# A PEER layer in fp32 on one core: 320 instead of 352 tokens computed densely, 192 gathered, and the gathers begun beside the gate matrices

## Chip, cores and metric

The kernel runs on one core of a Trainium2 chip. The metric is the device time of one execution in microseconds. Three runs of the kernel before took 3478.0, 3478.22 and 3481.24 us; the median is 3478.22 us.

## What is computed

One decoder layer over 512 tokens of 2048 features, all in float32: two groups of attention heads, an output projection with residual, then a PEER block and a final RMSNorm. The change concerns the PEER block alone:

```python
q = (xt @ w_query).reshape(T, PEER_HEADS, 2, PEER_HALF)          # 512 tokens, 8 heads, 2 x 128
scores = jnp.einsum('thpc,hpnc->thpn', q, sub_keys)              # 128 keys per half
vals, idx = lax.top_k(scores, 16)
cand = vals[..., 0, :, None] + vals[..., 1, None, :]             # 16 x 16 sums
top_vals, top_c = lax.top_k(cand, 16)                            # 16 experts per head
experts = i1 * 128 + i2                                          # of 16384 experts
gates = softmax(top_vals)
hdn  = gelu(einsum('ted,td->te', expert_down[experts], x))       # 128 experts per token
y    = einsum('te,ted->td', gates * hdn, expert_up[experts])
```

An expert is one row of 2048 numbers in `expert_down` and one in `expert_up`; each table has 16384 rows (134 MB).

## The kernel before, in words

**Two ways through the experts.** For the first `ND` = 352 tokens the kernel computes all 16384 experts densely, as 128 tiles of 128 experts, and multiplies the hidden values by a gate matrix that is zero where a token did not choose the expert. For the last 160 tokens it gathers the chosen rows: 128 tokens as part "g", one row per partition and step (128 steps in `down`, 128 in `up`), and `NE` = 32 tokens as part "e", four experts at a time on 4 x 32 partitions (32 steps in each table). That makes 320 gather steps of 128 rows of 8 KB, 1 MB each. Every matmul that is not a transpose, a gate matrix or a score runs as three passes over fp32 values split into a high and a low half (`mm3`, lines 96 to 98); ScalarE makes the high half (line 90), VectorE or GpSimd the low one (line 91, argument `lo_on`).

**The stages**, in the order of the program:

1. Attention and output projection, up to about 950 us. Not touched.
2. Routing (lines 494 to 549): per head two query projections `pq` of 48 matmuls, scores `sc`, then on VectorE top-16 of the scores, candidate sums, top-16 of those, and a one-hot product `oh` that turns positions into expert numbers, for all four blocks of 128 tokens; GpSimd takes every second `oh` product (line 537).
3. Gate matrices (lines 570 to 615): the tokens are handled in `NGC` = 11 chunks of 32. Per group of 8 tokens VectorE writes two comparisons `o2` and `o1` (lines 602, 603), GpSimd (two groups in three) or ScalarE multiplies `o1` by the gates, TensorE makes the matrices `gm` (line 612), ScalarE copies them to a staging tile, and a chunk of 2 MB is written to HBM (`g_d`).
4. Early `down` tiles (lines 738 to 742): 18 tiles (`SPILL`), whose hidden values go to HBM and are needed last, and 10 (`HOLD`) that stay in SBUF, both with the low halves on GpSimd. A scheduler moves part of their matmuls forward into stages 2 and 3.
5. The main loop (lines 745 to 786): 32 groups of 4 tiles. Per group the gate columns `gt` are loaded, the hidden values multiplied and split, and for each of 16 output chunks of 128 features 12 matmuls `up` are summed in PSUM and added to `yacc` by VectorE (line 773). After every fourth chunk's worth of work one later `down` tile is computed, with one low half on VectorE and one on GpSimd. `gather_step` (line 641 on) is called up to 12 times per group: GpSimd issues the indirect DMA into one of three buffers `rows` (line 650), held back until a named matmul has run, and VectorE multiplies what arrived (line 654 for `down`, 662 for `up`).
6. The end: residual, RMSNorm and output in the last group.

Each engine works through its own queue in order, and the order is fixed when the program is built. So where a gather's product stands in VectorE's queue, all that stands behind it waits for that gather's landing.

## Time and profile before

| | us |
|---|---|
| median of three runs | 3478.22 |
| profiled execution, its own time | 3480.87 |
| its span, first to last instruction | 3479.1 |
| TensorE matmuls busy | 3282.0 (94%) |
| VectorE busy | 2545.0 (73%) |
| GpSimd busy | 1183.5 (34%) |
| ScalarE busy | 1180.3 (34%) |

The profiled execution is 1.8 us longer than its span, and 2.65 us longer than the median. All stretches below are in microseconds from the start of the span. In the rows PE is TensorE's matmuls, PEld its weight loads, DVE VectorE, ACT ScalarE, POOL GpSimd and SP the queue that issues plain DMAs; L91 is line 91 of the kernel. PEclk is the granted clock of TensorE, 1.00 being 2.4 GHz.

### The profile page before, as it was taken

What the parts mean: (1) busy time and instruction counts of PE and PEld (TensorE: products, weight loads), DVE (VectorE), ACT (ScalarE), POOL (GpSimd) and SP (SyncE); (2) the same over time, 40 slices, a digit from 0 to 9 for tenths busy, and PEclk for the clock granted to TensorE, in tenths of its full rate; (3) what the DMA queues carried; (4) which work ended last, traced back from release to release, by engine and by line L of the source; (5) the groups of instructions that cost most, each with busy time, mean ns of one, the idle gap of its engine ahead of it and who ended that gap; (6) DMA issues with size and microseconds to landing.
All of it is one profiled execution on the core that took longest, in us unless ns stands there. A gap on an engine that the chain in (4) does not pass through costs nothing.

```text
span 3479.1 us, 47060 instructions
## 1 busy us (share of the span) xinstructions
PE 3282.0 (94%) x18329; PEld 3015.0 (87%) x18329; DVE 2545.0 (73%) x3652; ACT 1180.3 (34%) x1651; POOL 1183.5 (34%) x584
## 2 busy tenths in 40 slices
PE   6999999999998977899999999999999999998787
PEld 4887778878877766899999899999999999998787
DVE  5236664453469999127988889999999998998775
ACT  3224443342321267333333333333333333332133
POOL 2000000000054356454544445554554555552200
PEclk9999999999999999999999999999999999999899
DMA  4222222224332134547888889899898999988763
GB/s 179 93 93 68 70 76 68 69 89 138 123 137 75 46 130 162 196 151 299 339 329 342 308 339 352 344 344 353 330 358 335 346 345 348 346 344 318 283 199 108
DMA packets 207902, 780.35 MB, mean 224 GB/s; under 512 B 19648, under 2 KB 69696, under 8 KB 163456
## 3 DMA queue, kind: packets, MB, share of 16 engines
q1 hardware_dynamic: 160752, 440.35, 36.3%
q0 software_dynamic: 46080, 335.56, 24.4%
q8 instruction: 143, 2.34, 0.3%
q10 hardware_dynamic: 848, 1.44, 0.1%
q14 instruction: 79, 0.65, 0.1%
HBM read 739.70 MB, written 36.41 MB: 223 GB/s over the span
## 4 chain that ended last, share of the span: by engine, by line
PE 22%; DMA 18%; DVE 10%; issue 8%; POOL 1%; ACT 0%; DVEq 0%; POOLq 0%; ACTq 0%; SPq 0%
DMA rows<-in_up,gidx 12%; DMA rows<-in_down,gidx 5%; PE dn L96 4%; PE dn L98 4%; PE dn L97 4%; PE up L96 3%; PE up L97 3%; PE up L98 3%; DVE rows L654 3%; DVE yg_g L662 2%; DVE ulo L763 1%; DVE lo L91 1%; DVE yacc L773 1%; POOL rows L650 1%; DVE hn L755 1%
## 5 line engine op out<-in xcount | busy, mean ns | idle before, releaser
L91 POOL TENSOR_TENSOR lo<-raw,hi 128x1024 fp32r<-128x1024 f32 x186 | 483.0, 2599 | 762.1 <-ACT hi L90 744.1
L96 PE MATMUL up<-hn,ulo 128*128 128x352 f32 x2048 | 673.3, 329 | 55.5 <-DVE ulo L763 55.3
L90 ACT ACTIVATE hi<-raw 128x1024 fp32r<-128x1024 f32 x416 | 439.3, 1057 | 771.6 <-PE dn L98 279.5
L96 PE MATMUL dn<-hn,lo 128*128 128x352 f32 x2048 | 678.1, 331 | 22.3 <-POOL lo L91 11.1
L98 PE MATMUL dn<-hn,hi 128*128 128x352 f32 x2048 | 674.8, 329 | 0.0
L97 PE MATMUL dn<-hn,hi 128*128 128x352 f32 x2048 | 674.5, 329 | 0.0
L98 PE MATMUL up<-hn,uhi 128*128 128x352 f32 x2048 | 668.8, 327 | 0.0
L97 PE MATMUL up<-hn,uhi 128*128 128x352 f32 x2048 | 666.3, 325 | 0.0
L91 DVE TENSOR_TENSOR lo<-raw,hi 128x1024 fp32r<-128x1024 f32 x230 | 316.4, 1376 | 284.7 <-ACT hi L90 284.4
L762 ACT ACTIVATE uhi<-uraw 128x1024 fp32r<-128x1024 f32 x256 | 271.4, 1061 | 640.8 <-PE up L98 597.0
L96 PEld LDWEIGHTS up<-hn,ulo 128*128 128x128 f32 x2048 | 390.2, 191 | 62.8 <-DVE ulo L763 57.8
L96 PEld LDWEIGHTS dn<-hn,lo 128*128 128x128 f32 x2048 | 387.3, 189 | 36.0 <-POOL lo L91 17.6
L662 DVE SCALAR_TENSOR_TENSOR yg_g<-rows,coef_g,yg_g 128x2048 f32<-128x2048 f32 x127 | 348.7, 2745 | 66.3 <-DMA rows<-in_up,gidx 66.2
L97 PEld LDWEIGHTS up<-hn,uhi 128*128 128x128 f32 x2048 | 389.4, 190 | 0.0
L98 PEld LDWEIGHTS up<-hn,uhi 128*128 128x128 f32 x2048 | 388.1, 190 | 0.0
L98 PEld LDWEIGHTS dn<-hn,hi 128*128 128x128 f32 x2048 | 387.6, 189 | 0.5
L97 PEld LDWEIGHTS dn<-hn,hi 128*128 128x128 f32 x2048 | 386.7, 189 | 0.6
L654 DVE SCALAR_TENSOR_TENSOR rows<-rows,hng_g 128x2048 f32<-128x2048 f32 x128 | 322.6, 2526 | 47.0 <-DMA rows<-in_down,gidx 46.9
L763 DVE TENSOR_TENSOR ulo<-uraw,uhi 128x1024 fp32r<-128x1024 f32 x256 | 315.9, 1234 | 47.8 <-ACT uhi L762 47.5
L650 POOL DMA_INDIRECT rows<-in_up,gidx x128 | 227.6, 1778 | 168.5 <-PE up L98 88.1
L773 DVE TENSOR_TENSOR yacc<-yacc,up 128x352 f32<-128x352 f32 x496 | 246.0, 509 | 38.8 <-PE up L98 38.7
L650 POOL DMA_INDIRECT rows<-in_down,gidx x128 | 229.5, 1793 | 90.1 <-issue 41.3
(258 smaller groups left out, 4885.7 us busy)
## 6 DMA issues: line engine op xcount, KB each, us to landing
raw<-in_down_t SPq DMA_DIRECT2D x256, 512.0 KB
uraw<-in_up_t SPq DMA_DIRECT2D x256, 512.0 KB
raw<-in_w_qk SPq DMA_DIRECT2D x64, 512.0 KB
g_d<-stg SPq DMA_DIRECT2D x11, 2048.0 KB
gt<-g_d SPq DMA_DIRECT2D x32, 704.0 KB
raw<-in_w_v SPq DMA_DIRECT2D x32, 512.0 KB
raw<-in_w_o SPq DMA_DIRECT2D x32, 512.0 KB
raw<-in_w_pq SPq DMA_DIRECT2D x32, 512.0 KB
```

Source lines behind the costliest of these rows:

```text
L90: A.activation(hi, raw, AF.Copy)
L91: (lo_on or V).tensor_tensor(lo, raw, hi.bitcast(F32), ALU.subtract)
L96: PE.matmul(ps, a[1], b[0], start=first, stop=False)
L97: PE.matmul(ps, a[0], b[1], start=False, stop=False)
L98: return PE.matmul(ps, a[0], b[0], start=False, stop=last)
L650: ld = G.indirect_dma_start(out=rows, out_offset=None, in_=table, in_offset=bass.IndirectOffsetOnAxis(ap=ix[:, j:j + 1], axis=0))
L654: V.scalar_tensor_tensor(rows, rows, 1.0, hng[part], ALU.mult, ALU.mult, accum_out=dots[part][:, j:j + 1])
L662: V.scalar_tensor_tensor(yg[part], rows, coef[part][:, j:j + 1], yg[part], ALU.mult, ALU.add)
L755: V.tensor_tensor(pl, hold[e], ph.bitcast(F32), ALU.subtract)
L762: A.activation(uh, raw, AF.Copy)
L763: V.tensor_tensor(ul, raw, uh.bitcast(F32), ALU.subtract)
L773: V.tensor_tensor(yacc[:, c], yacc[:, c], ps[:, :ND], ALU.add)
```

## The change

Six things change together.

- `ND` goes from 352 to 320, `NE` from 32 to 64: the dense matmuls have 320 columns, there are 10 gate chunks, and part "e" has 64 steps per table, so that there are 384 gather steps.
- Routing is done in two halves of two blocks (`RB`): first blocks 2 and 3, which hold all gathered tokens, while the query projections run; the queries of blocks 0 and 1 are kept in SBUF and routed afterwards.
- The gather code moves out of the main loop's pool, and five gather steps (`PRE`) are called after each gate chunk, without a matmul to wait for.
- Early tiles: `SPILL` goes from 18 to 28, so 38 tiles are computed ahead instead of 28.
- The main loop has 16 groups of 8 tiles (`NG`): 24 matmuls per PSUM sum, half as many additions to `yacc`. The gate columns arrive in runs of 1 KB instead of 512 B, the `up` weights still in runs of 4 KB. A gather is due 1.6 times per output chunk of 24 matmuls while `down` tiles remain, and 0.85 times after that.
- In the main loop both low halves of a `down` tile are VectorE's.

```diff
-ND = 352
+ND = 320
-NE = 32
+NE = 64
+RB = 2
-SPILL = 18
+SPILL = 28
+NG = 8
+PRE = 5
...
+        def choose(hh, b0, queries):
+            bs = slice(b0, b0 + RB)
...
+        kept = rp.tile([P, 2 * PH, RB * P], F32, name="kept")
+        def queries(hp):
+            ps = aux(f"pq{hp}")
...
+            A.copy(qt, ps[:, RB * P:])
+            A.copy(kept[:, hp], ps[:, :RB * P])
+            return qt
+        for hh in range(PH):
+            choose(hh, NB - RB, queries)
...
+        for hh in range(PH):
+            choose(hh, 0, lambda hp: kept[:, hp])
...
-                o2 = gp.tile([P, QT, P], F32, name="o2", bufs=4)
-                o1 = gp.tile([P, QT, P], F32, name="o1", bufs=4)
+                o2 = gp.tile([P, QT, P], F32, name="o2", bufs=2)
+                o1 = gp.tile([P, QT, P], F32, name="o1", bufs=3)
...
             DMA.dma_start(g_d[ch], stg)
+            for _ in range(PRE):
+                gather_step(None)
...
-            for dc in range(8):
-                raw = xp.tile([P, NG, 256], F32, tag="uraw", name="uraw", bufs=3)
+            for c in range(NK):
+                raw = xp.tile([P, NG, P], F32, tag="uraw", name="uraw", bufs=3)
...
-                        down_tile(e, (V, G))
+                        down_tile(e, (V, V))
...
-                for _ in range(1 + (dc % 2 == 0) if HOLD + g * NG < NE1 - SPILL else 1):
+                due += 1.6 if e < NE1 - SPILL else 0.85
+                while due >= 1:
                     gather_step(mm)
+                    due -= 1
```

Three places in the order of the built programs show where work is moved.

The first is VectorE's queue in the middle of the gate stage. Before, only comparisons stand there (`o1` and `o2` are the tiles of lines 602 and 603):

```order
L602 TENSOR_TENSOR o2_9343<-iota_e_9034,i2t_9046 128x1024
L603 TENSOR_TENSOR o1_9344<-iota_e_9034,i1t_9045 128x1024
L602 TENSOR_TENSOR o2_9360<-iota_e_9034,i2t_9046 128x1024
L603 TENSOR_TENSOR o1_9361<-iota_e_9034,i1t_9045 128x1024
L602 TENSOR_TENSOR o2_9386<-iota_e_9034,i2t_9046 128x1024
L603 TENSOR_TENSOR o1_9387<-iota_e_9034,i1t_9045 128x1024
```

Now products of gathered rows (`rows15` is the gather of step 15) stand between them:

```order
L512 SCALAR_TENSOR_TENSOR rows15_9721,dots_e_6975<-rows15_9721,hng_e_9435 128x2048
L670 TENSOR_TENSOR o2_9696<-iota_e_9325,i2t_9328 128x1024
L512 SCALAR_TENSOR_TENSOR rows16_9724,dots_e_6975<-rows16_9724,hng_e_9435 128x2048
L512 SCALAR_TENSOR_TENSOR rows17_9727,dots_e_6975<-rows17_9727,hng_e_9435 128x2048
L512 SCALAR_TENSOR_TENSOR rows18_9730,dots_e_6975<-rows18_9730,hng_e_9435 128x2048
L670 TENSOR_TENSOR o2_9737<-iota_e_9325,i2t_9328 128x1024
L512 SCALAR_TENSOR_TENSOR rows19_9733,dots_e_6975<-rows19_9733,hng_e_9435 128x2048
L671 TENSOR_TENSOR o1_9738<-iota_e_9325,i1t_9327 128x1024
L670 TENSOR_TENSOR o2_9754<-iota_e_9325,i2t_9328 128x1024
L671 TENSOR_TENSOR o1_9755<-iota_e_9325,i1t_9327 128x1024
L671 TENSOR_TENSOR o1_9772<-iota_e_9325,i1t_9327 128x1024
L512 SCALAR_TENSOR_TENSOR rows20_9813,dots_e_6975<-rows20_9813,hng_e_9435 128x2048
```

Seven of the 50 products stand before the first comparison, four behind the last one, and 39 between the 80 comparisons.

The second is GpSimd's queue at the same place. Before, it holds the gate products and a few low halves of early tiles; now the issues of the gathers (L507) stand among them, each waiting for a free `rows` buffer, with the products (L673) and low halves (L94) queued behind:

```order
L507 DMA rows23_9822<-in_down,gidx_e_6963 128x2048
L673 TENSOR_TENSOR o1_9796<-o1_9796,gtt_9329 128x1024
L94 TENSOR_TENSOR lo_11437<-raw_11434,hi_11436 128x1024
L507 DMA rows24_9825<-in_down,gidx_e_6963 128x2048
L507 DMA rows25_9905<-in_down,gidx_e_6963 128x2048
L507 DMA rows26_9908<-in_down,gidx_e_6963 128x2048
L673 TENSOR_TENSOR o1_9830<-o1_9830,gtt_9329 128x1024
L507 DMA rows27_9911<-in_down,gidx_e_6963 128x2048
L673 TENSOR_TENSOR o1_9871<-o1_9871,gtt_9329 128x1024
L94 TENSOR_TENSOR lo_11471<-raw_11468,hi_11470 128x1024
```

From the first gate product to the last, this queue holds 26 products and 16 low halves now. Of the matmuls of the 38 early tiles (1824), 672 stand before the tables of the gate stage are transposed, 388 between them and the last `gm`, and 764 behind the last `gm`; before, 944 of 1344 stood behind it.

The third is TensorE's queue while the queries are projected. Before, five matmuls of an early tile stand between a query projection and its scores:

```order
L98 MATMUL pq2_7227<-hn0_6788,hi_7260 128x512
L96 MATMUL dn110_9965<-hn0_6788,lo_9999 128x352
L97 MATMUL dn110_9965<-hn1_6789,hi_9998 128x352
L98 MATMUL dn110_9965<-hn0_6788,hi_9998 128x352
L96 MATMUL dn110_9965<-hn0_6788,lo_9999 128x352
L97 MATMUL dn110_9965<-hn1_6789,hi_9998 128x352
L510 MATMUL sc2_7290<-sk_6974,qt_7288 128x128 x4
L96 MATMUL pq3_7323<-hn0_6788,lo_7327 128x512
```

Now the scores, for two blocks, stand right behind the projection whose result they wait for:

```order
L99 MATMUL pq2_7192<-hn0_6788,lo_7226 128x512
L100 MATMUL pq2_7192<-hn1_6789,hi_7225 128x512
L101 MATMUL pq2_7192<-hn0_6788,hi_7225 128x512
L556 MATMUL sc22_7256<-sk_6984,qt_7253 128x128 x2
L99 MATMUL pq3_7275<-hn0_6788,lo_7279 128x512
L100 MATMUL pq3_7275<-hn1_6789,hi_7278 128x512
```

## Rows read from the trace of the kernel before

**Rows 1.** Windows: busy us (instructions) of PE, PEld, DVE, ACT, POOL, PEclk, DMA share, GB/s

```profile
0.00:953.00 953.00, 917.34 (x4375) 730.71 (x4376) 455.08 (x875) 346.02 (x563) 23.17 (x28) 1.00 0.29 97
953.00:1224.00 271.00, 247.94 (x1122) 203.98 (x1121) 226.76 (x1007) 63.41 (x78) 128.57 (x55) 0.95 0.26 87
1224.00:1403.00 179.00, 133.64 (x891) 120.19 (x890) 173.57 (x107) 124.69 (x222) 103.38 (x38) 0.92 0.37 148
1403.00:1576.00 173.00, 162.36 (x949) 156.71 (x949) 27.82 (x23) 54.38 (x70) 90.83 (x38) 0.97 0.53 173
1576.00:3171.00 1595.00, 1579.66 (x9608) 1568.82 (x9607) 1451.38 (x1369) 508.58 (x610) 805.26 (x401) 1.00 0.90 340
...
3171.00:3479.00 308.00, 241.06 (x1394) 234.61 (x1392) 210.37 (x274) 83.21 (x112) 32.32 (x24) 0.90 0.61 211
```

**Rows 2.** Windows of 100 us: 352 columns in the main loop, 512 in the attention

```profile
2300.00:2400.00 100.00, 100.00 (x614) 99.72 (x613) 92.96 (x95) 31.27 (x37) 50.27 (x25) 1.00 0.88 339
100.00:200.00 100.00, 100.00 (x430) 80.47 (x429) 24.80 (x22) 21.49 (x22) 0.00 (x0) 1.00 0.30 94
```

**Rows 3.** Windows of the main loop, for the PEld and DMA columns

```profile
2200.00:2800.00 600.00, 599.60 (x3661) 597.14 (x3661) 556.41 (x541) 193.31 (x231) 311.39 (x153) 1.00 0.91 345
1680.00:1720.00 40.00, 40.00 (x245) 39.80 (x245) 38.00 (x42) 13.53 (x17) 17.54 (x11) 1.00 1.00 381
2840.00:2860.00 20.00, 20.00 (x125) 20.00 (x124) 18.92 (x17) 8.09 (x12) 9.34 (x5) 1.00 1.02 394
```

**Rows 4.** Timeline of the last projection and its scores: start us, us, instruction

```profile
1202.32 0.40 PE L98 MATMUL pq<-hn,hi 128*128 128x512 f32 x1
...
1202.81 0.59 ACT L507 COPY qt<-pq 128x512 f32<-128x512 f32 x1 [14.79 <-PE pq L98]
...
1203.45 1.16 PE L510 MATMUL sc<-sk,qt 128*128 128x128 f32 x8
```

**Rows 5.** Groups of the gate stage, 1224 to 1403 us: busy, mean ns, idle before

```profile
L603 DVE TENSOR_TENSOR o<-iota_e,i1t 128x1024 f32<-128x1024 f32 x44 | 103.1, 2344 | 0.8 <-ACT i1t L589 0.8
...
L605 POOL TENSOR_TENSOR o<-o,gtt 128x1024 f32<-128x1024 f32 x29 | 78.7, 2712 | 66.4 <-DVE o L603 35.1 <-PE gm L612 21.9 <-PE dn L98 4.7
L602 DVE TENSOR_TENSOR o<-iota_e,i2t 128x1024 f32<-128x1024 f32 x44 | 64.1, 1458 | 0.2 <-ACT i2t L589 0.2
...
L91 POOL TENSOR_TENSOR lo<-raw,hi 128x1024 fp32r<-128x1024 f32 x8 | 24.7, 3089 | 2.8 <-ACT hi L90 2.8
```

**Rows 6.** VectorE's timeline in the main loop

```profile
2302.16 1.21 DVE L763 TENSOR_TENSOR ulo<-uraw,uhi 128x1024 fp32r<-128x1024 f32 x1
2303.29 2.28 DVE L654 SCALAR_TENSOR_TENSOR rows<-rows,hng_g 128x2048 f32<-128x2048 f32 x1
...
2305.50 2.28 DVE L654 SCALAR_TENSOR_TENSOR rows<-rows,hng_g 128x2048 f32<-128x2048 f32 x1
...
2307.71 3.42 DVE L91 TENSOR_TENSOR lo<-raw,hi 128x1024 fp32r<-128x1024 f32 x1
2311.05 2.28 DVE L654 SCALAR_TENSOR_TENSOR rows<-rows,hng_g 128x2048 f32<-128x2048 f32 x1
```

**Rows 7.** GpSimd's timeline at the same time

```profile
2306.47 3.57 POOL L91 TENSOR_TENSOR lo<-raw,hi 128x1024 fp32r<-128x1024 f32 x1 [5.83 <-ACT hi L90]
```

**Rows 8.** The gathers' DMA queue over the whole run: packets, MB, share

```profile
q0 software_dynamic: 46080, 335.56, 24.4%
```

**Rows 9.** Groups of 3171 to 3310 us, where the last 20 gathers run

```profile
L96 PE MATMUL up<-hn,ulo 128*128 128x352 f32 x176 | 63.3, 360 | 38.0 <-DVE ulo L763 37.9
...
L751 DVE TENSOR_TENSOR hold<-hold,gt 128x352 f32<-128x352 f32 x3 | 1.5, 521 | 9.1 <-DMA hold<-hid_d 9.1
```

**Rows 10.** The tile `up` on TensorE: ns, first and last start

```profile
L96 PE MATMUL up<-hn,ulo x2048: 318/325/662, 1575.8 to 3461.1; 128*128 128x352 f32 x187
```

**Rows 11.** Timelines of the last gathers: an issue, and the product that waits for its landing

```profile
3212.28 0.94 POOL L650 DMA_INDIRECT rows<-in_up,gidx  x1 [1.43 <-DVE ulo L763]
...
3220.68 2.35 DVE L662 SCALAR_TENSOR_TENSOR yg_g<-rows,coef_g,yg_g 128x2048 f32<-128x2048 f32 x1 [2.01 <-DMA rows<-in_up,gidx]
```

More of the change, by code (lines that the diff above doesn't have):

```diff
@@ L470, in peer_block @@
     hold_p = ctx.enter_context(tc.tile_pool(name="hold", bufs=HOLD))
+    ga = ctx.enter_context(tc.tile_pool(name="gath", bufs=1))
+    hng = {}
+    sel = ga.tile([P, NE], F32, name="sel")
+    V.tensor_copy(sel, ident[:, 0:NE])
+    for r in range(1, ER):
+        V.tensor_tensor(sel, sel, ident[:, r * NE:(r + 1) * NE], ALU.add)
+    steps = [(w, part, j) for part, n in (("e", EH), ("g", HK)) for w in (down, up) for j in range(n)]
+    lists = {"e": (gidx_e, gate_e), "g": (gidx, top.rearrange("p b h k -> p b (h k)")[:, GB])}
@@ new lines, in peer_block, with gather_step @@
+    dots = {p: ga.tile([P, n], F32, name=f"dots_{p}") for p, n in (("e", EH), ("g", HK))}
+    coef = {p: ga.tile([P, n], F32, name=f"coef_{p}") for p, n in (("e", EH), ("g", HK))}
+    yg = {}
+    gstep = [0]
+    def gather_step(after):
+        n = gstep[0]
+        gstep[0] += 1
+        if n >= len(steps):
+            return
+        table, part, j = steps[n]
+        ix, gate = lists[part]
+        last = j == ix.shape[1] - 1
+        if n == 0:
+            hng["e"] = ga.tile([P, D], F32, tag="hy", name="hng_e")
+            for r in range(ER):
+                DMA.dma_start(hng["e"][r * NE:(r + 1) * NE], hn_d[:NE])
+        elif part == "g" and steps[n - 1][1] == "e":
+            hng["g"] = ga.tile([P, D], F32, tag="hy", name="hng_g")
+            DMA.dma_start(hng["g"], hn_d[NE:])
+        rows = ga.tile([P, D], F32, tag="rows", name=f"rows{n}", bufs=3)
+        ld = G.indirect_dma_start(out=rows, out_offset=None, in_=table,
+                             in_offset=bass.IndirectOffsetOnAxis(ap=ix[:, j:j + 1], axis=0))
+        if after is not None:
+            tc.add_manual_dep(ld.ins, after.ins.name, PACE, reason="pace")
+        if table is down:
+            V.scalar_tensor_tensor(rows, rows, 1.0, hng[part], ALU.mult, ALU.mult, accum_out=dots[part][:, j:j + 1])
+            if last:
+                A.activation(coef[part], dots[part], AF.Gelu_apprx_tanh)
+                V.tensor_tensor(coef[part], coef[part], gate, ALU.mult)
+        elif j == 0:
+            yg[part] = ga.tile([P, D], F32, tag="hy", name=f"yg_{part}")
+            V.tensor_scalar(yg[part], rows, coef[part][:, j:j + 1], None, ALU.mult)
+        else:
+            V.scalar_tensor_tensor(yg[part], rows, coef[part][:, j:j + 1], yg[part], ALU.mult, ALU.add)
+        if table is up and last:
+            fin_part(part)
@@ L683, in fin_load @@
                     fin[b, half] = t
[L684 removed]
+            fin["row"] = ga.tile([P, D], F32, tag="rows", name="frow", bufs=3)
             DMA.dma_start(fin["row"], fin_row.broadcast_to([P, D]))
@@ L774, in peer_block @@
-                if dc % 2:
-                    e = HOLD + g * NG + dc // 2
-                    if e < NE1 - SPILL:
-                        down_tile(e, (V, G))
-                    elif e < NE1:
+                ps = aux("up")
+                for j in range(NG):
+                    mm = mm3(ps[:, :ND], (uh[:, j], ul[:, j]), pp[j], j == 0, j == NG - 1)
+                if g == 0:
+                    V.tensor_copy(yacc[:, c], ps[:, :ND])
+                else:
+                    V.tensor_tensor(yacc[:, c], yacc[:, c], ps[:, :ND], ALU.add)
```

165 lines of the change are left out of this document (59 added, 106 removed).

## The prediction

> **What bounds the kernel now.** I read the windows by stage first, then the mean steps of TensorE, then what ends the waits in the stages that the change touches. The windows [rows 1] show three regimes. From 1576 to 3171 us, where two thirds of the matmuls run, TensorE is busy 1579.7 of 1595 us at full clock; VectorE (1451 us) and the DMA engines (0.90) are close behind. Between 953 and 1576 the bound changes: routing and gate matrices fill VectorE (227 of 271 us, 174 of 179), the early tiles fill TensorE while VectorE works 28 of 173 us. In the tail TensorE is busy 241 of 308 us.
>
> A matmul's price follows its columns [rows 2]: 100 us hold 614 matmuls of 352 columns, 0.163 us each, and 430 of 512 columns, 0.2326 each. That is 0.0697 us for 160 columns, so 320 columns should take 0.163 - 32 x 0.0697 / 160 = 0.149 us.
>
> **The change, part by part.** *Dense width.* 12288 matmuls (128 tiles, 48 in `down` and 48 in `up`) save 0.0139 us each: 171 us. This is all that the change can win; everything else gives back.
>
> *Front.* Nothing changes up to 953 us.
>
> *Routing in two halves.* While the queries of blocks 2 and 3 are routed, no other matmul stands between a projection and its scores, so TensorE waits for ScalarE's copy. In the timeline [rows 4] the last matmul of a projection starts at 1202.32, the scores at 1203.45: less one step of 0.23, the gap is 0.9 us with a 0.59 us copy, some 0.6 us where only half of the columns is copied first. With two scores at 0.145 (8 in 1.16) a projection takes 48 x 0.2326 + 0.6 to 0.9 + 0.3, about 12.3 us; 16 take 198: 1151. VectorE has half of its work in these 198 us and is hidden; its last piece I put at 15 us (one head of eight in 130). The second half is VectorE's alone. All four blocks took it from the first scores (953 and one projection, 965) to 1224, 259 us, so two take 130: 1296. The 672 early matmuls that stand there (100 us) are hidden in it.
>
> *Gates.* Ahead of the first comparison stand seven gathered products, 15 us, and the transposes of the tables, 5: the gates start at 1316, 92 us later than before. Their cost is VectorE's. An undisturbed comparison is one of 1024 elements, 1.13 us [rows 6] (2302.16 to 2303.29); a product is 2.21 (2303.29 to 2305.50). But the low half that ran while GpSimd worked [rows 7] (2306.47 to 2310.04) took 3.34. The gate stage shows the same [rows 5]: 88 comparisons took 103.1 + 64.1 = 167.2 us where 88 x 1.13 = 99.4 would do, 67.8 us over, 1.83 for each of the 37 GpSimd operations (29 products, 8 low halves). Now 80 comparisons (90), 39 products (86) and 42 GpSimd operations x 1.83 (77) make 253. Waits for landings come on top: an issue is followed by its product after 8.4 us [rows 11] (3212.28 to 3220.68), and with three buffers five gathers take at least 5 x (8.4 + 2.2) / 3 = 18 us of a chunk's 25, so they fit, but GpSimd's products are queued behind issues that wait for a buffer. I take 2 us per chunk, 273 in all; the bounds are none (253) and one landing of 8.4 with one GpSimd product of 2.7 [rows 5] exposed in each chunk, 36 us a chunk (360). The gates end at 1589, the last group passes TensorE at 1595, against 1403.
>
> *Early tiles.* Behind that stand 764 matmuls. Before, 944 took 173 us [rows 1] with the clock at 0.97 and 11 us idle: 764 x 0.149 / 0.97 + 11 = 128. The main loop starts at 1723 instead of 1576: **147 us of the 171 are given back here**, for ten tiles more computed ahead and 50 gathers done.
>
> *Main loop.* 90 tiles remain; I count in rounds of 8 tiles, 11.25 of them. A round holds 768 matmuls, 114.4 us. VectorE has 25.6 products x 2.2 (57), 32 halves x 1.13 (36, no GpSimd tensor operation disturbs them now) and 32 small operations at no more than the 0.52 us of such a one [rows 9] (17): 110. The DMA engines move 16.8 MB of weights, 1.3 of gate columns and 25.6 gathers of 335.56 / 320 = 1.049 MB [rows 8], 44.9 MB. That is 392 GB/s at TensorE's pace. Before, the loop needed 345 GB/s at a share of 0.91 [rows 3]; 40 us ran at 381 with the share at 1.00 and 20 us at 394 with 1.02, and TensorE lost nothing in them. So the full engines give about 381: **117.8 us per round, set by the DMA**. Bounds: 114.4 (394 held) and 130.2 (345 stays the average). I take 117.8, nearest to the longer of the full stretches. 11.25 x 117.8 = 1325, with 15 us of idle time as before: 3063.
>
> The Trainium skill ("DMA: Bandwidth & Descriptors", section "Where 436 GB/s comes from") puts the limit of transfers between HBM and SBUF at about 358 GB/s per core. By it a round would take 125.5 us and the end would come near 3527. The 381 and 394 GB/s of the rows lie above that figure, though only over 40 and 20 us.
>
> *Tail.* 76 chunks of 24 matmuls are 272 us. Before, the tail of 308 us held 1344 `up` matmuls (219 us), 18 us behind the last one [rows 10] (3461.1 to 3479.1), and 71 us lost, 38 of them behind VectorE's low halves that stand behind gathers [rows 9]. Twenty gathers ran there, now 46 do; at half of 8.4 / 3 us exposed each (1.4) they cost 64, the wait for stored hidden values (9.1 before [rows 9]) 10, the last part 15: 89. Bounds: 71 as before, and 46 x 2.8 + 25 = 154. 3063 + 361 + 18 = **3442 us** of span, 37 less than 3479.1. The profiled execution is 1.8 us longer than its span and 2.65 over the median of the runs, so the median should come to 3441.
>
> Half as many sums to `yacc` and longer runs of the gate columns I cost at nothing: VectorE and TensorE are not the bound of a round at 117.8. If they were (110 and 114.4) they would be late next.
>
> **Rivals.**
>
> *Slower: the transfers do not keep 371 GB/s.* The gain of 37 us is gone when a round takes 37 / 11.25 = 3.3 us more, 121.1 us, 371 GB/s. Place: the three `rows` buffers in the main loop. A round at 117.8 has 4.6 us per gather, 13.8 for a buffer's turn; 8.4 + 2.2 + about 1 us to the next issue leave 2.2 us. If full DMA engines make a landing later than that (over 10.9 us), VectorE stops at the product, the low halves behind it stop, and TensorE with them. For it: 345 GB/s over 600 us is the longest stretch shown, and VectorE is within 8 us of the round. Against: in the two full stretches [rows 3] TensorE was busy throughout. At 345 to 365 GB/s a round takes 130 to 123 us, the end is 3500 to 3581. A limit that shows only in long stretches, between the 345 shown over 600 us and the 381 over 40, would give the same: at 355 to 365 GB/s 123 to 126.5 us, 3500 to 3540; I give it 0.12 of this rival's 0.25, since no row shows full engines below 381.
> The figure of the skill's section above lies in that span.
>
> *All fits.* The engines hold 394 GB/s, a round is TensorE's 114.4, 38 us less; with gates at 253 the end is 3383 to 3403. For it: TensorE's idle time is 15 us in 1595 now. Against: three engines would all be over 95% busy.
>
> *The gates are longer.* 36 us per chunk instead of 27 add 87 us: 3528. For it: GpSimd's issues wait for buffers ahead of its gate products. Against: 18 us of landings fit beside 25 us of VectorE's work in a chunk. Half of this rival would end within 0.2% of before.
>
> *No price falls with the columns.* The weight loads are busy 597 of 600 us [rows 3]; if they set the pace, the matmul stays at 0.163 and 171 us are missing: 3612. Against: at 512 columns there is one load per matmul too, and they are busy only 80% of the time [rows 2]; the busy time stretches with the matmul.
> The Trainium skill ("Perfetto Trace Analysis", section "Identifying the Most-Contended Engine") judges TensorE's headroom by the busy share of the weight loads; by it 99.5% would leave none.
>
> That the change does not do what it says the order of the built program excludes: the dense matmuls have 320 columns there and the 39 products stand between the comparisons.
>
> **How the numbers follow.** The forecast with its own spread (3395 to 3470) has 0.41; all fits 0.14; a mixture that ends within 0.2% of 3478, about what a measurement of this kernel can tell from no change, 0.12; transfers too slow 0.25; gates too long 0.05; no price by columns 0.03. Faster is 0.41 + 0.14 = 0.55, same 0.12, slower 0.33. The likeliest time is 3441 us; its own range is 3395 to 3470. Eight in ten must reach into both neighbours: 3385 leaves 0.08 below, 3540 leaves 0.12 above (the slower part of the slow transfers and the last rival).
>
> **What the profile would show.** Right: `dn` and `up` matmuls 0.149 us apart; the last scores of blocks 2 and 3 near 1151; the first `o2` near 1316, the last `gm` near 1595, the first `up` near 1723; 16 chunks of `up` every 118 us at a DMA share of 1.00 and about 381 GB/s; the last down tile near 3063. Wrong: a share under 0.95 with TensorE waiting for `ulo` or `lo` behind gathered products (three buffers too few), a DMA rate that stays at 345 to 358 with the share at 1.00, a chunk of gates over 30 us, or a tail over 400 us.

## The result, and the profile after

The changed kernel takes 3585.29 us (median of four runs, 3585.21 to 3585.91) against 3479.73 for the kernel before beside it. The ratio is 1.0303, with an interval from 1.0285 to 1.0321: **slower by 3.0%**. The forecast was 3441 with a range from 3385 to 3540. The profiled execution took 3585.91 us, its span is 3584.1.

First the stages of the changed kernel, to be held against [rows 1] (the windows view; its columns are those of [rows 1]):

```profile
953.00:1339.00 386.00, 324.31 (x1583) 274.43 (x1582) 274.32 (x1194) 104.52 (x146) 192.42 (x85) 0.93 0.35 120
1339.00:1646.00 307.00, 173.84 (x1029) 165.50 (x1030) 254.66 (x158) 128.97 (x214) 212.40 (x84) 0.78 0.62 230
1646.00:1770.00 124.00, 118.18 (x763) 113.47 (x763) 35.49 (x27) 44.03 (x58) 74.29 (x31) 1.00 0.60 208
1770.00:3178.00 1408.00, 1320.01 (x8650) 1301.93 (x8650) 1206.88 (x1157) 446.98 (x548) 424.39 (x288) 0.97 0.94 359
3178.00:3567.00 389.00, 306.85 (x1862) 297.99 (x1861) 275.51 (x288) 100.62 (x133) 56.43 (x48) 0.89 0.73 264
```

The lines are routing (up to the first gate matrix `gm`), gates, the early tiles behind them, the dense loop up to the last `down` matmul, and the tail up to the last `up`. The loop begins at 1770 instead of 1576 us (194 later), is 187 us shorter, and the last `up` starts 389 us behind it instead of 290 (99 more): 106 us in all. The prediction's 1316 was the first comparison of the gates. It starts at 1334.77, 4 us ahead of the first `gm` at which the window is cut (start, us, instruction):

```profile
1334.77 1.22 DVE L671 TENSOR_TENSOR o<-iota_e,i1t 128x1024 f32<-128x1024 f32 x1
```

Against the sum of the prediction the differences are:

| | forecast, us | measured | difference |
|---|---|---|---|
| front and routing, up to the first comparison | 1316 | 1335 | +19 |
| gates, up to the last `gm` | 279 | 311 | +32 |
| early tiles | 128 | 125 | -3 |
| dense loop | 1340 | 1408 | +68 |
| tail, up to the last `up` | 361 | 389 | +28 |
| behind it | 18 | 17 | -1 |

They make the 142 us from 3442 to 3584, but for rounding. The largest part is the loop, so I looked there first. The waits of its 1408 us (engine, line, what it waited for: us in total, times, longest):

```profile
POOL rows L507 <- PE up L101: 604.2, 100, 17.4
...
DVE rows L512 <- DMA rows<-in_down,gidx: 69.0, 60, 4.3
...
PE dn L99 <- DVE lo L94: 46.6, 30, 9.8
...
DVE yg_g L520 <- DMA rows<-in_up,gidx: 40.6, 33, 3.6
...
PE up L99 <- DVE ulo L788: 39.3, 19, 9.6
...
DVE yg_e L520 <- DMA rows<-in_up,gidx_e: 33.9, 27, 3.4
...
DVE hold L776 <- DMA gt<-g_d: 26.8, 7, 10.1
...
DVE rows L512 <- DMA rows<-in_down,gidx_e: 7.9, 9, 2.1
```

TensorE waits for VectorE's low halves, and VectorE waits at products for rows that have not landed: 69.0 + 40.6 + 33.9 + 7.9 = 151 us. Its work is 1207 us; with these stops and 27 us for the gate columns it is 1385 of 1408. The reading that the experiments below test is: **VectorE's queue, not the DMA engines, is what the loop takes.** The DMA engines stand at a share of 0.94, under the 1.00 that the forecast wanted. One place in VectorE's timeline (start, us, instruction) shows how a stop reaches TensorE:

```profile
2109.38 2.35 DVE L520 SCALAR_TENSOR_TENSOR yg_e<-rows,coef_e,yg_e 128x2048 f32<-128x2048 f32 x1
2111.65 0.48 DVE L776 TENSOR_TENSOR hold<-hold,gt 128x320 f32<-128x320 f32 x1
2114.09 2.35 DVE L520 SCALAR_TENSOR_TENSOR yg_e<-rows,coef_e,yg_e 128x2048 f32<-128x2048 f32 x1 [1.96 <-DMA rows<-in_up,gidx_e]
2116.36 0.48 DVE L795 TENSOR_TENSOR yacc<-yacc,up 128x320 f32<-128x320 f32 x1
2116.76 1.22 DVE L94 TENSOR_TENSOR lo<-raw,hi 128x1024 fp32r<-128x1024 f32 x1
2117.89 1.22 DVE L788 TENSOR_TENSOR ulo<-uraw,uhi 128x1024 fp32r<-128x1024 f32 x1
```

The product at 2114.09 stands still for 1.96 us, and behind it in the same queue stand the `lo` and `ulo` that TensorE needs next. TensorE stood 0.67 us for that `lo`:

```profile
2118.03 0.41 PE L99 MATMUL dn<-hn,lo 128*128 128x320 f32 x1 [0.67 <-DVE lo L94]
```

A second reading, which I should have made beforehand: the same view of the kernel before, over its loop from 1576 to 3171:

```profile
DVE yg_g L662 <- DMA rows<-in_up,gidx: 47.0, 37, 2.4
DVE rows L654 <- DMA rows<-in_down,gidx: 46.9, 31, 6.4
DVE rows L654 <- DMA rows<-in_down,gidx_e: 17.3, 11, 2.1
DVE yg_e L662 <- DMA rows<-in_up,gidx_e: 16.7, 10, 2.7
```

These are 128 us of stops. With the 1451 us of work in [rows 1] VectorE's queue held 1579 of the loop's 1595 us, as much as TensorE. That is a warning and not yet a bound: a stop also grows when another engine sets the pace, as the run with the halved product shows below.

In the gates the groups from 1310 to 1646 us answer to [rows 5]:

```profile
L512 DVE SCALAR_TENSOR_TENSOR rows<-rows,hng_e 128x2048 f32<-128x2048 f32 x46 | 132.4, 2899 | 51.5 <-DMA rows<-in_down,gidx_e 51.5
L671 DVE TENSOR_TENSOR o<-iota_e,i1t 128x1024 f32<-128x1024 f32 x40 | 73.2, 1846 | 0.0
L670 DVE TENSOR_TENSOR o<-iota_e,i2t 128x1024 f32<-128x1024 f32 x40 | 71.0, 1778 | 2.9 <-PE gm L680 2.5 <-ACT i2t L657 0.4
...
L94 POOL TENSOR_TENSOR lo<-raw,hi 128x1024 fp32r<-128x1024 f32 x20 | 74.2, 3723 | 0.0
L673 POOL TENSOR_TENSOR o<-o,gtt 128x1024 f32<-128x1024 f32 x26 | 72.4, 2788 | 54.4 <-DVE o L671 45.6 <-PE dn L99 4.7 <-PE gm L680 2.4
```

The 80 comparisons took 144.2 us, 53.8 over 80 x 1.13; the 46 products 132.4, 30.7 over 46 x 2.21. That is 84.5 us for 46 GpSimd operations, 1.84 each; the forecast took 1.83. One place shows such a hold, a product of 3.98 instead of 2.28 us that starts while a GpSimd operation runs up to 1460.03 (a line each of GpSimd's and VectorE's timeline):

```profile
1457.29 2.74 POOL L673 TENSOR_TENSOR o<-o,gtt 128x1024 f32<-128x1024 f32 x1 [0.43 <-DVE o L671]
...
1458.20 3.98 DVE L512 SCALAR_TENSOR_TENSOR rows<-rows,hng_e 128x2048 f32<-128x2048 f32 x1
```

The stops at landings are 51.5 us where the forecast took 20.

### The profile page after: what moved, and what is told of

The parts are those of the page before. It is cut to its first block, busy times and chain, and to the rows that moved or that the text cites. A ratio compares the mean times of both kernels' runs of the same rounds, so it can differ in the third digit from the quotient of the medians.

```text
span 3584.1 us, 47019 instructions
## 1 busy us (share of the span) xinstructions
PE 3162.2 (88%) x18265; PEld 2885.4 (81%) x18265; DVE 2508.8 (70%) x3713; ACT 1176.2 (33%) x1669; POOL 985.4 (27%) x565
## 4 chain that ended last, share of the span: by engine, by line
PE 35%; DMA 27%; DVE 17%; issue 15%; POOL 5%; ACT 1%; DVEq 0%; ACTq 0%; SPq 0%; POOLq 0%
DMA rows<-in_up,gidx 8%; DMA rows<-in_down,gidx 7%; DMA rows<-in_down,gidx_e 4%; DMA rows<-in_up,gidx_e 4%; DMA gt<-g_d 3%; PE mm L101 3%; PE mm L100 3%; PE mm L99 3%; DVE rows L512 3%; POOL lo L94 3%; DVE yg_g L520 2%; DVE ulo L788 2%; DVE lo L94 2%; PE po L99 2%; PE po L101 2%
## 5 line engine op out<-in xcount | busy, mean ns | idle before, releaser
L99 PE MATMUL up<-hn,ulo 128*128 128x320 f32 x2048 | 657.5, 321 | 113.3 <-DVE ulo L788 110.4
L99 PE MATMUL dn<-hn,lo 128*128 128x320 f32 x2048 | 658.4, 321 | 83.8 <-DVE lo L94 46.6
L100 PE MATMUL up<-hn,uhi 128*128 128x320 f32 x2048 | 651.3, 318 | 9.9 <-DVE hn L780 9.9
L100 PE MATMUL dn<-hn,hi 128*128 128x320 f32 x2048 | 650.8, 318 | 0.0
L101 PE MATMUL up<-hn,uhi 128*128 128x320 f32 x2048 | 650.0, 317 | 0.0
L101 PE MATMUL dn<-hn,hi 128*128 128x320 f32 x2048 | 647.8, 316 | 0.0
L94 DVE TENSOR_TENSOR lo<-raw,hi 128x1024 fp32r<-128x1024 f32 x310 | 379.2, 1224 | 280.8 <-ACT hi L93 280.5
L520 DVE SCALAR_TENSOR_TENSOR yg_g<-rows,coef_g,yg_g 128x2048 f32<-128x2048 f32 x127 | 298.3, 2349 | 86.5 <-DMA rows<-in_up,gidx 85.8
L94 POOL TENSOR_TENSOR lo<-raw,hi 128x1024 fp32r<-128x1024 f32 x106 | 287.5, 2716 | 186.4 <-ACT hi L93 184.8
L507 POOL DMA_INDIRECT rows<-in_up,gidx x128 | 177.3, 1385 | 515.5 <-PE up L101 353.0
L507 POOL DMA_INDIRECT rows<-in_down,gidx x128 | 179.3, 1401 | 454.6 <-PE up L101 267.4
L680 PE MATMUL gm<-o,o 128*128 128x128 f32 x640 | 114.4, 352 | 131.6 <-POOL o L673 69.1
```

Of the source, the lines that this page charges most:

```text
L94: (lo_on or V).tensor_tensor(lo, raw, hi.bitcast(F32), ALU.subtract)
L99: PE.matmul(ps, a[1], b[0], start=first, stop=False)
L100: PE.matmul(ps, a[0], b[1], start=False, stop=False)
L101: return PE.matmul(ps, a[0], b[0], start=False, stop=last)
L507: ld = G.indirect_dma_start(out=rows, out_offset=None, in_=table, in_offset=bass.IndirectOffsetOnAxis(ap=ix[:, j:j + 1], axis=0))
L520: V.scalar_tensor_tensor(yg[part], rows, coef[part][:, j:j + 1], yg[part], ALU.mult, ALU.add)
```

## The experiments

Two theories for the loop stood first. **Q**: VectorE's queue (its work and its stops at products) is the loop. **R**: the DMA engines give no more than some 359 GB/s over a long stretch. Later came the questions why VectorE stops, and what each part of the change is worth. Unless a row says otherwise a time is one run, set against the changed kernel's 3585 and the kernel before's 3481 to 3482 beside it; four runs are timed in rounds. Ten runs of one of these kernels (the first of the two in rounds further down) lie between 3470 and 3491 us, so differences of less than some 20 us between single runs are not clear of noise. "Loop" is from the first `up` to the last `down` matmul.

### Bytes or VectorE

```diff
-                DMA.dma_start(raw, up_t[g, c])
+                if c % 2 == 0:
+                    DMA.dma_start(raw, up_t[g, c])
```

> The changed kernel, but only every second load of the up weights is issued in the dense loop (the two chunks of a pair use the same loaded tile, so half of the up products are of other weights); every operation of TensorE, VectorE, ScalarE and GpSimd stays. A round of 8 tiles then moves 40.7 MB instead of 44.9. Theory Q (VectorE's queue stops at products whose rows have not landed; the loop is its busy time plus those stops): the loop from the first up matmul to the last down matmul stays within 40 us of the 1408 of the changed kernel, the DMA rate falls to about 325 GB/s. Rival R (the DMA engines give some 359 GB/s over long stretches and no more): the loop falls with the bytes to TensorE's pace, about 1300 us, and the rate stays near 355.

3527.9 us; the loop took 1372 us at 335 GB/s. A tenth fewer bytes took 36 us off the loop, where R wanted 110.

```diff
-            V.scalar_tensor_tensor(rows, rows, 1.0, hng[part], ...
+            V.scalar_tensor_tensor(rows[:, HF], rows[:, HF], 1.0, hng[part][:, HF], ...
```

(`HF` is the first half of the columns; the same in the `up` products.)

> The changed kernel, but the product of a gathered row uses its first 1024 of 2048 elements (the gathered tokens' result lacks the other half); all transfers and all other operations stay. VectorE has 25.6 x 1.1 = 28 us less per round of 8 tiles. Theory Q (VectorE's queue): the loop of 1408 us falls to 1290 to 1340, and the DMA rate rises to 375 to 390 GB/s. Rival R (a rate of 359 GB/s is the limit): the loop stays at 1390 to 1410 and the rate at 359.

3391.9 us, 193 less with every byte still moved. The gates, the early tiles and the loop in the windows view:

```profile
1328.90:1540.90 212.00, 130.75 (x759) 122.88 (x760) 177.01 (x158) 115.21 (x198) 146.02 (x71) 0.77 0.79 301
1540.90:1726.80 185.90, 166.25 (x1060) 160.08 (x1059) 37.30 (x29) 59.75 (x78) 105.84 (x46) 0.96 0.55 190
1726.80:3025.00 1298.20, 1284.36 (x8646) 1276.94 (x8646) 912.93 (x1157) 445.18 (x548) 342.24 (x289) 1.00 0.99 390
```

The DMA engines carry 390 GB/s for 1298 us and TensorE is busy 99% of them. R falls, Q stands. Two limits go with it. A halved product also frees its buffer some 1.1 us sooner, so this run does not tell VectorE's work from the turn of the three buffers. And VectorE's stops at landings rise to 333 us:

```profile
DVE rows L513 <- DMA rows<-in_down,gidx: 150.1, 88, 5.1
DVE yg_g L522 <- DMA rows<-in_up,gidx: 85.6, 55, 4.1
DVE yg_e L522 <- DMA rows<-in_up,gidx_e: 75.7, 45, 3.1
...
DVE rows L513 <- DMA rows<-in_down,gidx_e: 21.3, 13, 2.5
```

With its 913 us of work VectorE's queue holds 1246 of 1298 us although TensorE now sets the pace: work plus stops fills a loop even where the engine is not its bound. Ahead of the loop the gates lose 95 us, but the early tiles behind them take 61 more, as fewer of them ran beside the gates; the first `up` starts 43 us earlier.

### Why VectorE stops

```diff
-                    gather_step(mm)
+                    gather_step(back)
...
+                back = mm
```

> The changed kernel, but in the dense loop a gather is held back by the last matmul of the output chunk before, not of this chunk, so it may be issued about 7 us earlier. The time from a free buffer to the issue was 2.1 us on average, of which about 0.3 is the engine's own. Theory Q with the hold as its cause: the turn of a buffer falls from 14.8 to 13 us, the stops at products (152 us in the loop) fall by half, the loop to 1320 to 1360. Theory Q with the number of buffers as its cause: a buffer is free no earlier, the loop stays within 30 us of 1408. Rival R (DMA rate): stays within 15 us.

3580.9 us, loop 1404: the earlier permission alone does nothing. Whether a free buffer is what is missing was tried next.

```diff
-        rows = ga.tile([P, D], F32, tag="rows", name=f"rows{n}", bufs=3)
+        rows = ga.tile([P, D], F32, tag="rows", name=f"rows{n}", bufs=4)
...
-HOLD = 10
+HOLD = 9
```

(and two buffers for `uraw` and for `o1` instead of three)

> The changed kernel with four buffers of gathered rows instead of three; to make room for them the dense loop has two buffers of raw up weights instead of three, nine held tiles instead of ten, and the gates two buffers for o1 instead of three. Theory B (three buffers set the gathers' pace: a turn of 2.1 to the issue, 8.4 to the landing, 1.9 in VectorE's queue and 2.3 for the product is 14.7 us, 4.9 per gather): the landings' stops of 152 us in the loop mostly go, the loop falls from 1408 to 1280 to 1330, the time to 3460 to 3500. Rival O (the place of the product in VectorE's queue, set when the program is built, decides, and VectorE is full anyway): the loop stays at 1380 or over.

> The kernel of the run with four buffers, but with three of them: two buffers of raw up weights, nine held tiles, two for o1. It shows what the room taken away costs by itself. If the smaller buffers cost nothing: within 15 us of the changed kernel, 3570 to 3600. If they cost: up to 60 us more, and the run with four buffers is read against this one.

With four buffers 3489.2 us, but the same room with three gives 3508.5. The fourth buffer itself is worth 19 us between two single runs, and 8 in the loop (1377 against 1385), where B wanted 78 or more: theory B falls. The surprise is that *less* room made the kernel 77 us faster. Two of the three edits were run alone:

```diff
-                raw = xp.tile([P, NG, P], F32, tag="uraw", name="uraw", bufs=3)
+                raw = xp.tile([P, NG, P], F32, tag="uraw", name="uraw", bufs=2)
```

> The changed kernel with two buffers of raw up weights instead of three and nothing else changed; one of the three edits that together took 77 us off. If the third buffer is what costs (loads of weights issued far ahead queue in front of the gathers): loop and tail 25 to 45 us shorter, time 3540 to 3560. If it is not: within 10 us of 3585.

3582.1 us: nothing.

```diff
-                o1 = gp.tile([P, QT, P], F32, name="o1", bufs=3)
+                o1 = gp.tile([P, QT, P], F32, name="o1", bufs=2)
```

> The changed kernel with two buffers for o1 instead of three and nothing else changed; the second of the three edits. If o1's third buffer is what costs in the gates (comparisons run ahead, GpSimd's products then meet the gathered products on VectorE): last gm at about 1620 instead of 1646, time 3545 to 3565. If it is not: the gates take 300 us or more and the time stays within 10 us of 3585.

3544.4 us, 41 less: the gates take 283 instead of 307, the early tiles 119, the loop 1396. The other 33 us of the 77 belong to the ninth held tile or to the edits together; that was not separated.

```diff
+        pend.append(lambda: product(rows, table, part, j, gate, last))
+        if len(pend) > LAG:
+            pend.pop(0)()
```

(`LAG` = 2, on the kernel with four buffers)

> The kernel of the run with four buffers (two raw up buffers, nine held tiles, two o1), but the product of a gather is written in the program two gathers later than its issue, so that it stands later in VectorE's queue. Theory P (the product's place in the queue causes the stops): landings' stops in the loop fall from about 120 us to under 50, the loop from 1377 to 1290 to 1330, the time from 3489 to 3400 to 3450. Rival T (the buffers' turn is full either way: a product that stands later frees its buffer later): the stops go to other places, the loop stays within 25 us of 1377.

3478.9 us, 10 less than with four buffers; loop 1370, stops 132 us. This does not test theory P: in the two traces the products of gathers 60 to 330 stand at nearly the same place of VectorE's queue, on average 0.04 `yacc` additions later. The program's text was changed, the queue's order hardly. In these two kernels a buffer stood free for 6 us before its next issue, which waited for the chunk's matmul; so hold and buffers were then eased together (the edit of the earlier issue on the kernels with four buffers):

> The kernel of the run with four buffers, and a gather held back by the last matmul of the output chunk before instead of this chunk: both limits on the issue are eased together. Theory J (hold and buffers each keep the issue late when the other is eased): a row is issued up to 5 us earlier, the landings' stops in the loop fall from about 120 us to under 50, the loop from 1377 to 1290 to 1330, the time from 3489 to 3400 to 3445. Rival K (the products move up in VectorE's queue with the issue, so the stop moves with them): stops over 90 us, the loop within 25 us of 1377.

> As the run before in this list, and each product written two gathers later in the program. Theory J: the stops go as there, or more: loop 1280 to 1330, time 3390 to 3440. Rival K holds and the queue's place follows the program: only this run has its stops under 60 us and its loop under 1340, the other not. If neither moves, the stops aren't a matter of issue, buffers or place, and stay open.

The first: 3481.4 us in rounds, ratio to before 0.9992 (0.9978 to 1.0006), loop 1373, stops 123 us: **K**, not J. The traces show K's mechanism: against the kernel with four buffers the issues come one output chunk earlier, and the products stand 0.99 `yacc` additions earlier in VectorE's queue, so a buffer still stands free for 6 us and the stop stays. (The earlier issue on three buffers moved its products by 0.99 too.) The second, with later products: 3439.0 us, ratio 0.9882 (0.9863 to 0.9901). Its loop, and VectorE's waits in it:

```profile
1713.90:3059.20 1345.30, 1307.53 (x8743) 1297.11 (x8742) 1217.28 (x1169) 447.69 (x554) 491.44 (x293) 0.99 0.98 381
```

```profile
DVE rows L523 <- DMA rows<-in_down,gidx: 38.0, 34, 2.6
...
DVE yg_e L531 <- DMA rows<-in_up,gidx_e: 21.1, 16, 3.9
DVE yg_g L531 <- DMA rows<-in_up,gidx: 16.7, 23, 1.6
...
DVE rows L523 <- DMA rows<-in_down,gidx_e: 10.8, 8, 2.4
```

The stops fall to 87 us. The sizes that the expectation gave for stops and loop were not met (under 60, under 1340), but the direction is clear. Of the combinations that were run only this one, a fourth buffer with an earlier issue and later products, lowers the stops that far; the others left 123 us or more. Later products without the fourth buffer were not run, and here too the products stand only 0.13 `yacc` additions later than in the first of the two kernels. A buffer stands free for 4 instead of 6 us. Why this helps so much is not shown.

### What the parts are worth

The width alone, on the kernel before:

```diff
-ND = 352
+ND = 320
-NE = 32
+NE = 64
...
-                for _ in range(1 + (dc % 2 == 0) if HOLD + g * NG < NE1 - SPILL else 1):
+                for _ in range(1 + (dc % 2 == 0)):
```

> The kernel before with the change of width alone: 320 tokens dense, 64 in part e, and 1.5 gathers per half group throughout, so that all 384 are done; routing, gates, 28 early tiles, four tiles per sum, low halves as before. Theory V (a gather costs VectorE more than its token's matmuls cost TensorE once VectorE is near full): the loop stays near VectorE's 1451 us of work plus its stops, 1530 to 1570 instead of 1595, the gates give 15 us, the tail with 84 instead of 20 gathers takes 60 us or more longer: 3440 to 3500. Rival W (the matmuls set the time, as in the sum of the prediction): 3479 - 171 + 40 = 3330 to 3380.

3570.1 us, **88 slower than before**. W falls; V's loop is right, its tail too short:

```profile
1549.00:3111.50 1562.50, 1470.67 (x9607) 1457.31 (x9606) 1443.84 (x1395) 502.02 (x610) 838.73 (x401) 0.97 0.91 346
3111.50:3537.70 426.20, 256.79 (x1381) 246.71 (x1381) 337.16 (x316) 72.91 (x94) 97.27 (x84) 0.80 0.80 294
```

9600 matmuls that are 0.0139 us shorter took 32 us off the loop instead of 133, for VectorE's 1444 us of work (and 97 of stops) remain; and the 64 more gathers made the tail 136 us longer, 2.1 us each.

The changed kernel at the old width (352 and 32, nine held tiles for room):

> The changed kernel with the width of before: 352 tokens dense, 32 in part e (nine held tiles, for room); everything else of the change stays, so 55 gathers stand beside 11 gate chunks and the other 265 fit in the dense loop. Theory V: the loop has 8640 matmuls of 0.163, 1408 us, and VectorE about 110 us of 125 per round, so the loop is as long as the changed kernel's, 1400 to 1440, while the tail has no gathers left and takes 300 to 330 instead of 389; the gates with 11 chunks 320 to 340: 3530 to 3570, below the changed kernel's 3585. Rival W (the narrower matmuls are the gain that other parts give back): 3585 + 100 or more.

3589.0 us. With eight tiles per sum and 352 columns the hidden values have seven slots, so here, and in the run at 352 columns with nine held tiles further down, the eighth tile's values take the place of the first's. Work and transfers are those of the full kernel. The loop is longer than V had it (1472, TensorE busy 1443), the tail as long as expected (304), and the time is neither V's (up to 3570) nor W's (3685 or more): beside all the other parts the width is worth 4 us, which is within the noise.

The front as before (routing at once, no gather ahead of the loop, the gate stage's buffers as before, 1.3 gathers per chunk in the tail):

```diff
-RB = 2
+RB = 4
-PRE = 5
...
-            for _ in range(PRE):
-                gather_step(None)
...
-                due += 1.6 if e < NE1 - SPILL else 0.85
+                due += 1.6 if e < NE1 - SPILL else 1.3
```

> The changed kernel with its front as before: all four blocks routed at once, no gather ahead of the dense loop, the buffers of the gate stage as before; 320 columns, 38 early tiles, eight tiles per sum, both low halves on VectorE and 1.6 gathers per chunk stay; 1.3 instead of 0.85 gathers per chunk in the tail, so that all 384 are done. Theory F (the halves and the gathers beside the gates cost more ahead of the loop than their 50 gathers cost in the loop and the tail): first up at 1600 to 1640 instead of 1770, the loop as now, 1390 to 1430, the tail with 96 gathers 450 to 490: 3500 to 3545. Rival V (50 gathers cost 4.9 us each wherever they run, so the place is no matter): 3570 to 3610.

3574.0 us. The first `up` comes at 1620, 150 earlier, and the loop takes 1421, but the tail with 96 gathers 509: F is right ahead of the loop and in it, but the sum is V's. Of the 150 us, 133 come back in loop and tail, 2.7 for each of the 50 gathers, not the 4.9 of V's reason. (This run undoes the routing in halves as well, so the 150 us are not the gathers' alone.) Gathers moved behind the gates instead (`PRE` = 0, two behind each of the last 16 early tiles, 1.7 in the loop):

> The changed kernel, but no gather in the gate stage; two gathers after each of the last 16 early tiles, held back by the tile's last matmul, and 1.7 instead of 1.6 gathers per output chunk in the loop. The gates should cost what they did before, 10/11 of 179 us plus 7 transposes and waits: the last gm at 1490 to 1520 instead of 1646; the early tiles behind it as long as now or a little longer, the first up matmul at 1630 to 1660 instead of 1770; the loop 1.7/1.6 longer where the gathers set it, 1408 to 1475; the time 3500 to 3540. If the gathers beside the gates cost nothing there, the first up comes at 1740 or later and the time at 3580 or more.

3604.6 us: the gates end at 1474, the first `up` starts at 1588, and the loop takes 1601, in part because 409 early matmuls now stand in it. **In all three places the 50 gathers are paid for.** One low half on GpSimd in the loop, as before the change (`down_tile(e, (V, G))`):

> The changed kernel with one of the two low halves of a down tile in the loop on GpSimd, as before the change. VectorE has 90 x 1.13 = 102 us less of its own and, at 2 us for each GpSimd tensor operation beside it, up to 180 us more of being held up. If that price holds where VectorE is the bound: the loop 40 to 80 us longer, 3620 to 3665. If VectorE's holding up falls into its stops: the loop 40 us or more shorter, 3545 or less.

3590.6 us, loop 1410: between the two expectations. VectorE's work rose by 65 us (90 halves fewer, 102 us, and 167 for 90 GpSimd operations beside it, 1.86 each), its stops fell from 151 to 115.

Last, the conclusion from these runs as a kernel: 352 columns and the front as before, 18 spilled tiles, the loop of the change (eight tiles, both halves on VectorE, 1.6 gathers). First with nine held tiles:

> The kernel before with the main loop of the change: 352 tokens, routing and gates as before, 18 early spilled and nine held tiles, but eight tiles per sum, both low halves on VectorE and 1.6 gathers per chunk of 24 matmuls, so that all 320 gathers are done before the tail. Theory V (VectorE's work per round decides): a round has 110 us of VectorE and 14 of stops against TensorE's 125, so the loop keeps TensorE's pace, 1580 to 1620 from 1570, and the tail falls from 290 to 230 to 250 us: 3415 to 3450. Rival: stops and work do not fit into 125 us, the loop takes 1650 or more: 3470 or more.

3442.8 us, as V had it; loop 1637 (V: up to 1620), tail 228. Then complete, with two raw up buffers and ten held tiles:

```diff
+    px = tuple(yp.tile([P, ND], F32R, name=f"px{i}") for i in range(2))
...
-        pslot, npslot = 0, (NTC - NGC) * NK * GC // ND
+        pslot, npslot = 0, NG
...
+                ph, pl = px if pslot == NG - 1 else (...
```

> The kernel before with 352 tokens dense, eight tiles per sum, both low halves on VectorE and 1.6 gathers per chunk, as in the run of this mixture, now with ten held tiles, two raw up buffers, and an eighth slot for hidden values, so that every tile's values are kept. Nothing of its work per round differs from that run: 3430 to 3455, faster than the kernel before by 0.7 to 1.4 per cent. If the eighth tile's own slot adds waits: 3460 or more.

3448.4 us over five rounds, ratio to before 0.9911 (0.9898 to 0.9925). Its loop and tail:

```profile
1562.10:3179.40 1617.30, 1587.31 (x9607) 1579.57 (x9607) 1356.91 (x1280) 498.93 (x606) 452.53 (x321) 0.99 0.91 347
3179.40:3422.90 243.50, 225.12 (x1379) 222.52 (x1379) 137.81 (x189) 77.77 (x106) 1.61 (x2) 0.96 0.55 178
```

The gain lies in the tail, where no gather is left (243 us against 290 before); the loop, with all 320 gathers in it, is 22 us longer than before. And with fewer gathers in the loop:

```diff
-                due += 1.6 if e < NE1 - SPILL else 0.85
+                due += 1.45 if e < NE1 - SPILL else 0.55
```

> The kernel of the run before in this list with 1.45 instead of 1.6 gathers per chunk in the loop and 0.55 instead of 0.85 in the tail, where some 30 of the 320 gathers then run. Theory V: a round of VectorE falls by 2.4 x 2.2 + stops, so TensorE sets the loop alone and it is 20 to 40 us shorter; the tail, whose VectorE is idle for 100 us, grows by 5 to 20: 3415 to 3440. Rival: the stops of the loop cost TensorE nothing at 352 columns and the tail's gathers are exposed: 3450 to 3470.

3466.0 us, ratio 0.9961 (0.9948 to 0.9975): the loop gains 22 us (1596 against 1617), the tail loses 27, and 12 more are lost behind the last `up` (31 us against 18). That is the rival's time, not V's. Gathers in the tail are not free though VectorE has time there. Its loop:

```profile
1566.90:3162.50 1595.60, 1575.28 (x9608) 1569.61 (x9607) 1293.97 (x1256) 499.19 (x606) 424.88 (x290) 1.00 0.88 334
```

With ten gathers fewer in it than the kernel before, VectorE has 1294 us of work here instead of 1451, and the loop is as long as before. So at 352 columns TensorE sets the loop, and VectorE's queue is the next bound close behind.

So the kernel before is beaten by the loop of the change at the old width (0.9911; 0.9961 with fewer gathers in the loop) and by the change with its gathers' issue, buffers and products re-arranged (0.9882): gains of about one per cent.

## Why the prediction was wrong

- **Price of a matmul: right.** The first 110 us of the loop hold 748 matmuls, 0.147 us each; the forecast had 0.149.

```profile
1770.00:1880.00 110.00, 110.00 (x748) 110.00 (x747) 89.45 (x87) 37.20 (x46) 33.67 (x24) 1.00 0.94 360
```

  The weight loads are busy all 110 us and yet the step fell from 0.163 of [rows 2]: the rival in which no price falls with the columns is out. The rule of the Trainium skill that stood beside it ("Perfetto Trace Analysis", section "Identifying the Most-Contended Engine") judges headroom by that share and by the share of the peak FLOP/s; the share alone would have left none, and the measured step decides against that reading here.
- **Routing, early tiles: right** (last scores of blocks 2 and 3 at 1158 for 1151; 125 us for 128). The gates begin 19 us late.
- **Gates: right in mechanism, short by 32.** GpSimd's hold on VectorE came out as priced, 1.84 us; the stops at landings were 51.5 instead of 20.
- **Dense loop, the step that failed: "117.8 us per round, set by the DMA".** A round took 1408 / 11.25 = 125.1 us. VectorE's work in it was 107.3 us, near the 110 of the forecast, but the forecast gave no time to its stops at landings: 13.5 us per round, and 2.4 for gate columns, 123.2 in all. I compared busy times of engines and took the largest; a queue in order also takes its waits. The halved product (loop 1298 at 390 GB/s) shows that neither DMA engines nor TensorE held the round at 125. TensorE lost 88 us of the loop idle, and its matmuls were busy 1320 us where 8650 at 0.147 are 1272: behind its waits the granted clock averaged 0.97, against 1.00 in the first 110 us, where it did not wait.
- **The limit of 358 GB/s** ("DMA: Bandwidth & Descriptors", section "Where 436 GB/s comes from" in the Trainium skill) is not this kernel's: 390 GB/s ran for 1298 us. Another section of the Trainium skill ("Perfetto Trace Analysis", section "Roofline") says that a single core can pull more than that share, and the trace agrees.
- **Tail: short by 28** of 389 us. 46 gathers ran there, and TensorE waited 71 us for `ulo`. It was idle 82 us, less than the 89 of the forecast; but at a granted clock of 0.89 its matmuls took 307 us where the forecast had 272. The forecast put the loss on gathers, stored values and the last part, and gave the slower clock no term.
- **The slower rival named the place and missed the cause.** It had VectorE stopping at products in the loop, from landings later than 10.9 us under full engines. By the packets of the gathers' queue a landing took 8.6 us on average from its issue, 9.1 before, and 8% took over 10.9, before 16%: landings did not come later than before, and VectorE stopped all the same. A buffer's turn took 14.7 us (2.1 to the issue, 8.6 to the landing, 1.7 more to the product, 2.3 for it), against the 13.8 that the rival had room for. Three buffers make the turn three periods long whatever sets the period, so these parts alone do not say which of them does.
- **"All that the change can win", 171 us, was not there to be won.** TensorE set the old loop, but VectorE's queue stood right behind it: the width alone won 32 us in the loop, not 133, and lost 88 in all. The 64 gathers that replace 32 columns were paid there with 136 us of tail. What the other parts cost depends on the width. At 352 columns the new loop takes 3443 to 3448 us with the old front and 3589 with the changed one, so that halves, early gathers and ten more early tiles cost 141 to 146 us. At 320 columns putting the front back won only 11, since the tail then took the gathers. Most of these are single runs, and the parts of the front were not taken apart further.

What stays open: why the stops fell only with buffer, issue and product changed at once, whether a product that really stands later in VectorE's queue would help by itself, and how much of the 77 us from smaller buffers belongs to the ninth held tile.

## What to carry to other kernels

Before work is moved from a full engine to the next one, look at the waits inside that engine's own queue as well as at its busy time. If the two together fill the span, it may be the next bound, whatever its busy share says. The sum does not prove it, since stops also grow when another engine sets the pace (913 + 333 us in the loop of the halved product). A run that changes one engine's work does: shorter matmuls that shorten the loop by 32 instead of 133 us, or VectorE's work cut by 157 us without a shorter loop. Price a gather by what moved gathers cost in the stage that takes them (here 2.1 to 2.7 us each, about the whole of their product, 2.3), not by the room that an engine's busy share seems to leave. And halving the suspected operation's size with all transfers left in place is a cheap way to tell an engine's queue from a DMA limit.

## What the runs showed of the hardware

- One core's DMA engines moved 390 GB/s at a share of 0.99 over 1298 us, beside TensorE at 99% (the run with the halved product).
- A GpSimd tensor operation held VectorE up by 1.84 us on average in the gates and 1.86 in the loop, with two different sets of VectorE operations beside it. The Trainium skill ("SBUF — State Buffer", section "SBUF: two separate sides") describes a port pair that the two engines take in turn for a whole instruction, and the trace agrees: the product that started at 1458.20 beside a GpSimd operation that ended at 1460.03, 1.83 us later, took 1.70 us more than its 2.28.
- One buffer less for `o1` took 41 us off the kernel in a single run, 24 of them in the gates, where GpSimd operations hold up VectorE; that fewer buffers can be faster was not expected, and why it is so was not shown.
